# The GELU branch of a recurrent mixer, computed token-major and placed between convolution tiles

## The chip, the cores and the metric

The kernel runs on one core of one Trainium2 chip. The metric is the device time of one execution in microseconds (us). Five engines each run their own queue of instructions in order: TensorE (PE: matmuls; PEld are its weight loads), VectorE (DVE), ScalarE (ACT), GpSimd (POOL) and SyncE (SP, which issues the DMA transfers here).

## The reference

An encoder trunk of two residual layers on 256 tokens of width 2048, in float32. Layer 0 mixes tokens with grouped-query attention, layer 1 with the recurrent block that the change concerns; behind each stands a gated feed-forward of width 5632.

```python
def recurrent_mixer(h, w_in, conv_w, conv_b, w_a, b_a, w_i, b_i, lam, w_out):
    xy = h @ w_in
    xb, yb = jnp.split(xy, 2, axis=-1)
    yb = jax.nn.gelu(yb, approximate=True)
    xb = depthwise_conv_centred(xb, conv_w, conv_b)
    h_fwd = rg_lru(xb, w_a[0], b_a[0], w_i[0], b_i[0], lam[0], reverse=False)
    h_bwd = rg_lru(xb, w_a[1], b_a[1], w_i[1], b_i[1], lam[1], reverse=True)
    out = (h_fwd + h_bwd).astype(h.dtype) * yb
    return out @ w_out
```

`rg_lru` takes the convolved branch `x` through two block-diagonal products with biases (blocks of 256 channels) to the gates r and i, forms a = sigmoid(lam)^(8 r) and u = sqrt(1 - a^2) (i x), and runs h_t = a_t h_(t-1) + u_t over the tokens, forward and backward.

## The kernel before

Matmuls run on pairs of tiles: each float32 operand is split into a rounded part `hi` and the rest `lo`, and three products (hi hi, hi lo, lo hi) make one float32 product. Weights come in halves of a tile, 128 x 1024 elements: SP loads `raw`, ACT casts it to `hi` (L116), DVE subtracts to `lo` (L117). There are five buffers of each. The list `order` fixes the sequence of all halves, and each call of `half()` loads the next.

A product is made in one of two layouts. Feature-major (`project_sum`): the weights are the stationary operand, the 256 tokens move, so that a matmul has 256 columns; the result has one feature per partition, as convolution, gates and scans over the tokens need it (48 matmuls for a tile of 128 features). Token-major (`project_tokens`): the activations are stationary and 512 features move ("wide", 96 matmuls for the two accumulators of a group of 512 features); the feed-forward and the output projections use it. Its results are turned back by 32 x 32 transposes on DVE and moves between partitions (`turned`).

The PE program is written out in code order. Besides the main stream there is a list of things to be done later: each group of matmuls calls `step()`, which advances a count, and `later(n, fn)` runs `fn` when the count has advanced by n, one at each step. In the feature-major tiles a step is three matmuls; in the token-major ones three wide matmuls make two steps. The order on ACT, DVE, POOL and SP is not written out: a scheduler puts it together from the program with a timeline of its own, and it is fixed once the kernel is built.

The recurrence has eight blocks of 256 channels (two tiles). Loop b projects and convolves the two x tiles of block b+1 (`conv_branch`: `cb` is the projection times the norm's factor, then one activation on ACT (L671) and three taps and a split on DVE end in `xs`), then projects the two GELU tiles of block b (`gelu_branch`). Among these stand, by the table `WHEN`, the rest of block b: the gates (`gates`, 12 matmuls each that read `xs`, then sigmoids and tanh), `decay` (exponentials and squares), `scan` (square root and scan), the GELU's table function, and `finish` (product and split into the operand tile `g_t` of the output projection). `WHEN_LAST` does it for the last block, where nothing is convolved any more. The first convolution is done by `project_two`, whose last quarter comes after both tiles' first parts. The norm's factor per token is brought to all partitions by `spread` with a small matmul (L336), `NORM` steps after it is asked for. The output projection (`output`) takes four column groups of eight halves; in the first, the last half is run after the pending work is flushed.

In the attention the last three heads have delays of their own (`LATE`), and the last one uses DVE in place of POOL.

Of the kernel before, what the change touches and what calls it, by code (L numbers as in the profile page):

```python
# [12 lines left out]
F32 = mybir.dt.float32  # L13
F32R = mybir.dt.float32r
# [18 lines left out]
COMMON = {"sq", "nsq", "nr", "nrt", "rsq_s", "nj", "ndg", "nrb"}  # L33
# [6 lines left out]
NORM = 26  # L40
# [29 lines left out]
def trunk(ctx, tc, w, out):  # L70
# [56 lines left out]

    def ffn_order(l):
# [82 lines left out]
    def project_tokens(xs, ready=0, close=None):  # L211
        accs = [new_acc() for _ in range(2)]
        for k0 in range(0, len(xs), 2):
            if close is not None and k0 == ready:
                flush()
                close()
            half()
            hi, lo = (t.rearrange("p (k c) f -> p k (c f)", k=2) for t in newest["tiles"])
            end = k0 + 2 == len(xs)
            for k, a in ((0, 0), (1, 0), (0, 1), (1, 1)) if end else ((0, 0), (0, 1), (1, 0), (1, 1)):  # L220
                xh, xl = (xs[k0 + k][:, o + a * P : o + (a + 1) * P] for o in (0, S))
                for n, (x, wt) in enumerate(((xh, hi), (xh, lo), (xl, hi))):
                    pe.matmul(  # L223
                        accs[a], x, wt[:, k, :], start=(k0 + k == 0 and n == 0), stop=(end and k == 1 and n == 2)
                    )
                step()
                step()
        return accs
# [16 lines left out]


    def project_two(xs, late):
        banks = [new_acc() for _ in range(2)]
        for t in banks:
            sums(t[:, :S], half(), xs, 0)  # L250
        rest = [half() for _ in range(2)]
        n = len(xs) - HALF - late
        for t, wt in zip(banks, rest):
            sums(t[:, :S], wt[:n], xs, HALF)
        for t, wt in zip(banks, rest):
            sums(t[:, :S], wt[n:], xs, HALF + n)
            yield t[:, :S], t[:, S:]
# [37 lines left out]
    class Norm:  # L295
# [17 lines left out]
        def add(self, c):  # L313
            for a in range(2):
                act.activation(tmp("nj", (P, WIDE), bufs=1), x_tok[:, a, c, :], AF.Square, accum_out=self.sums[:, a, c : c + 1])
            for f in turned(x_tok[:, :, c, :]):
                self.operand(f, True)
# [25 lines left out]

    def turned(src):
        b = fp[0].tile([P, 2, FOUR, P], F32, tag="tb", name=nm("tb"))
        f = fp[0].tile([P, 8, FOUR, 32], F32, tag="tf", name=nm("tf"))
        for a in range(2):
            dve.transpose(b[:, a, :, :], src[:, a, :])  # L348
# [27 lines left out]
    def output(xs, norm=None, end=False, ready=0, close=None):  # L376
        for c in range(NCOL):
            accs = project_tokens(xs, ready, None if c else close)
            for a, acc in enumerate(accs):
                n = 2 if end and c == NCOL - 1 else 1  # L380
                for i in range(n):
                    sl = slice(i * WIDE // n, (i + 1) * WIDE // n)
                    y = x_tok[:, a, c, sl]
                    dve.tensor_tensor(y, y, acc[:, sl], ALU.add)
                    if end:
                        sync.dma_start(out=out[:, a, c, sl], in_=y)
            if norm is not None:
                norm.add(c)
        if norm is not None:
            norm.finish()  # L390
# [137 lines left out]
    def attend(h, acc, dst):  # L528
        late = h >= NQ - 1
        eng = dve if late else pool  # L530
        d_sum, d_sc, d_turn, d_val = LATE[h - NQ] if h >= NQ - 3 else USUAL if h else FIRST_HEAD
# [3 lines left out]
        rope_sum(y, rope[0], q, eng)  # L535
# [16 lines left out]
        def scores():  # L552
# [16 lines left out]
            for a in range(2):  # L569
                eng.tensor_scalar(pr[:, a, :], pr[:, a, :], rs[:, a : a + 1], 1.0, ALU.mult, ALU.mult)  # L570
# [25 lines left out]
    def act_tile():  # L596
        return xp.tile([P, 2 * S], F32R, tag="act", name=nm("act"), bufs=18)
# [34 lines left out]
    output(o_t, nf, ready=KT - 2, close=end_attention)  # L632
# [31 lines left out]
    def conv_branch(ct, accs):  # L664
        acc, run = accs
# [36 lines left out]
    class Block:  # L702
        def __init__(self, b):
            self.b = b
            self.eng = pool if b < NBLK - 1 else dve
            self.xcs, self.ys = [], []
            self.gate, self.th, self.hs = {}, {}, {}

        def gelu(self):
            for y in self.ys:  # L710
                table_act(y, y, AF.Gelu_apprx_tanh)
# [43 lines left out]
        def finish(self, j):  # L755
            y = self.ys[j]
            dve.tensor_tensor(y, self.hs[j], y, ALU.mult)
            split(g_t[2 * self.b + j], y)
# [3 lines left out]
    blk = nxt = None  # L762
    for b in range(-1, NBLK):
        blk, nxt = nxt, Block(b + 1) if b + 1 < NBLK else None
        if blk:
# [3 lines left out]
            work += [blk.gelu] + [partial(blk.finish, j) for j in range(2)]  # L769
# [9 lines left out]
        if blk:  # L779
            blk.ys = [gelu_branch(2 * b + i) for i in range(2)]  # L780
# [8 lines left out]
    output(g_t, nf, ready=KT - 2, close=end_recurrence)  # L789
# [86 lines left out]
```

## Time and profile before

| | |
|---|---|
| median of 3 runs | 2037.25 us (2036.8 to 2037.25) |
| profiled execution | 2036.59 us, span 2034.8 us |
| busy: PE, DVE, ACT, POOL | 2021.0, 1311.9, 1157.2, 168.6 us |
| mean granted clock of TensorE | 0.998 |
| DMA | 386.02 MB, mean 190 GB/s |
| the recurrent mixer, from its first convolution to the start of its output projection | about 985.8 to 1225.9 us |

Times on the timeline count from the span's start. A row of it gives the start, the length, the engine, the line and the tile written and those read. A stretch gives busy time and number of instructions of PE, PEld, DVE, ACT and POOL, the clock granted to TensorE as a share of full speed, the share of the DMA engines and GB/s. The program's names are those of the code: `acc` and `pm` are accumulators, `xg` normed inputs, `act` operand tiles of the output and down projections.

### The profile page before, as it was taken

Reading aid. Unit: us, or ns where it says so; the run is one execution under the profiler, and the core shown is the slowest. Engines: PE = TensorE matmul, PEld = TensorE weight load, DVE = VectorE, ACT = ScalarE, POOL = GpSimd, SP = SyncE. Lnnn points to the kernel's source line nnn. Section 1 sums busy time; section 2 is a strip of 40 time slices with the busy share of each in tenths; the row PEclk is TensorE's granted clock in tenths of the full one; section 3 lists DMA queues with packets and bytes.
Section 4 is the critical chain, followed back from the end, with each engine's and each line's share of the span. In section 5 each row is a group of like instructions: output and inputs, shape, how many; then the busy total and the mean of one; then the engine's idle time right before and its main releaser. Section 6 shows DMA issues by size and latency. Waiting matters only on the chain.

```text
span 2034.8 us, 27445 instructions
## 1 busy us (share of the span) xinstructions
PE 2021.0 (99%) x10124; PEld 1722.5 (85%) x10124; DVE 1311.9 (64%) x1899; ACT 1157.2 (57%) x1776; POOL 168.6 (8%) x213
## 2 busy tenths in 40 slices
PE   9999999999999999999899999999999999999999
PEld 8898888888888888888799998888888888888887
DVE  7998765654665445667778987765555556555553
ACT  7665755544555345556689987755435554355442
POOL 1563000000000000000134330000000000000000
PEclk9999999999999999999999999999999999999999
DMA  8444565665666656666556555566666666666664
GB/s 319 157 135 145 186 202 193 186 203 191 187 197 197 195 195 193 186 199 196 188 165 188 187 157 194 180 205 197 190 194 195 193 190 196 196 189 195 197 202 129
DMA packets 108998, 386.02 MB, mean 190 GB/s; under 512 B 12224, under 2 KB 12992, under 8 KB 108736
## 3 DMA queue, kind: packets, MB, share of 16 engines
q1 hardware_dynamic: 108720, 384.26, 59.7%
q8 instruction: 79, 1.29, 0.3%
q14 instruction: 55, 0.45, 0.1%
q10 hardware_dynamic: 144, 0.02, 0.0%
HBM read 382.13 MB, written 2.10 MB: 189 GB/s over the span
## 4 chain that ended last, share of the span: by engine, by line
PE 54%; issue 40%; DVE 2%; DMA 2%; ACT 1%; POOL 0%; SPq 0%; DVEq 0%; POOLq 0%
PE acc L223 40%; PE acc L201 3%; PE acc L231 3%; PE acc L232 3%; PE acc L233 3%; PE pm L232 1%; PE pm L233 1%; PE pm L231 1%; DVE lo L117 1%; DMA x_tok<-in_xt_dram 1%; DMA graw<-in_w_gates_dram 0%; DMA raw<-in_w_k_dram 0%; PE pm L576 0%; DMA raw<-in_w_qv_dram 0%; ACT hi L116 0%
## 5 line engine op out<-in xcount | busy, mean ns | idle before, releaser
L117 DVE TENSOR_TENSOR lo<-raw,hi 128x1024 fp32r<-128x1024 f32 (+1 forms) x708 | 868.7, 1230 | 665.5 <-ACT hi L116 657.1
L116 ACT CAST hi<-raw 128x1024 fp32r<-128x1024 f32 (+1 forms) x708 | 739.4, 1047 | 751.7 <-PE acc L223 744.0
L223 PE MATMUL acc<-hi,xg 128*128 128x512 f32 x2816 | 867.8, 389 | 0.0
L223 PEld LDWEIGHTS acc<-hi,xg 128*128 128x128 f32 x2816 | 528.6, 188 | 109.6
L223 PE MATMUL acc<-hi,act 128*128 128x512 f32 x1920 | 594.2, 389 | 0.0
L223 PE MATMUL acc<-lo,xg 128*128 128x512 f32 x1408 | 547.7, 389 | 0.0
L223 PEld LDWEIGHTS acc<-hi,act 128*128 128x128 f32 x1920 | 360.4, 188 | 74.4
L223 PE MATMUL acc<-lo,act 128*128 128x512 f32 x960 | 373.5, 389 | 0.0
L223 PEld LDWEIGHTS acc<-lo,xg 128*128 128x128 f32 x1408 | 264.3, 188 | 54.9
L223 PEld LDWEIGHTS acc<-lo,act 128*128 128x128 f32 x960 | 180.2, 188 | 37.1
L231 PE MATMUL acc<-xg,hi 128*128 128x256 f32 x512 | 145.0, 283 | 0.0
L232 PE MATMUL acc<-xg,hi 128*128 128x256 f32 x512 | 145.0, 283 | 0.0
L233 PE MATMUL acc<-xg,lo 128*128 128x256 f32 x512 | 144.7, 283 | 0.0
L201 PE MATMUL acc<-xg,hi 128*128 128x512 f32 x384 | 125.8, 396 | 0.2 <-ACT hi L116 0.2
L354 ACT COPY tf<-tb 32x256 f32<-32x256 f32 x272 | 109.8, 404 | 3.7 <-DVE tb L348 0.2
L231 PEld LDWEIGHTS acc<-xg,hi 128*128 128x128 f32 x512 | 98.3, 192 | 0.0
L232 PEld LDWEIGHTS acc<-xg,hi 128*128 128x128 f32 x512 | 98.2, 192 | 0.1
L233 PEld LDWEIGHTS acc<-xg,lo 128*128 128x128 f32 x512 | 98.2, 192 | 0.0
L201 PEld LDWEIGHTS acc<-xg,lo 128*128 128x128 f32 x384 | 71.8, 188 | 16.0 <-DVE lo L117 1.9
L201 PE MATMUL acc<-xg,lo 128*128 128x256 f32 x384 | 84.8, 288 | 0.5 <-DVE lo L117 0.4
L356 DVE COPY tf<-tb 32x256 f32<-32x256 f32 x272 | 77.2, 284 | 4.0
L667 POOL MEMSET cb<- 128x2 f32 x16 | 1.7, 108 | 823.1 <-PE acc L233 811.6
(172 smaller groups left out, 1324.5 us busy)
## 6 DMA issues: line engine op xcount, KB each, us to landing
raw<-in_w_gate_dram SPq DMA_DIRECT2D x176, 512.0 KB, 4.0
raw<-in_w_up_dram SPq DMA_DIRECT2D x176, 512.0 KB, 3.9
raw<-in_w_down_dram SPq DMA_DIRECT2D x176, 512.0 KB, 3.8
raw<-in_w_in_dram SPq DMA_DIRECT2D x64, 512.0 KB, 4.3
raw<-in_w_qv_dram SPq DMA_DIRECT2D x40, 512.0 KB, 4.2
raw<-in_w_o_dram SPq DMA_DIRECT2D x32, 512.0 KB, 3.6
raw<-in_w_out_dram SPq DMA_DIRECT2D x32, 512.0 KB, 4.0
graw<-in_w_gates_dram SPq DMA_DIRECT2D x32, 256.0 KB, 3.4
```

The costliest lines, as they stand in the source:

```text
L116: newest["cast"] = act.copy(hi[:, sl, :], raw[:, sl, :])
L117: dve.tensor_tensor(lo[:, sl, :], raw[:, sl, :], hi[:, sl, :].bitcast(F32), ALU.subtract)
L201: pe.matmul(o, w, x, start=(k == 0 and not part), stop=(k == total - 1 and not part))
L223: pe.matmul(accs[a], x, wt[:, k, :], start=(k0 + k == 0 and n == 0), stop=(end and k == 1 and n == 2))
L231: pe.matmul(o, hi, x[:, :S], start=start, stop=False)
L232: pe.matmul(o, hi, x[:, S:], start=False, stop=False)
L233: pe.matmul(o, lo, x[:, :S], start=False, stop=stop)
L354: act.copy(o, y)
L356: dve.tensor_copy(o, y)
L667: pool.memset(b[:, 0:2], 0.0)
```

## The change

1. The GELU branch becomes token-major: `w_y`, the second half of `w_in`, is laid out in groups of 512 features, projected by the new class `Columns` (`project_tokens` in resumable form), and given the norm's factor in the activation. Its result is turned by two DVE transposes and 16 small DMAs on SP for each group. The multiplication by `nr.r` on DVE goes.
2. The first group is projected ahead of everything, before the first convolution; the others in two halves, each at the start of a loop, ahead of the convolution tiles of the next block. `project_two` goes.
3. In the loop of the last block but one, the half column is the first of the output projection; both output projections begin two column groups (seven halves each) before the pending work is flushed.
4. `LATE` goes; `NORM`, the tables `WHEN` and `WHEN_LAST`, some buffers and the order of weights are adapted.

```diff
-COMMON = {"sq", "nsq", "nr", "nrt", "rsq_s", "nj", "ndg", "nrb"}
+COMMON = {"sq", "nsq", "nr", "nrt", "rsq_s", "ndg", "nrb"}
-NORM = 26
+NORM = 30
-LATE = ((17, 22, 15, 12), (10, 23, 15, 13), (7, 16, 16, 9))
+GELU = 9
-WHEN = (18, 25, 32, 39, 42, 46, 50, 54, 58, 60, 62, 64, 66, 70, 74)
-WHEN_LAST = (5, 9, 13, 17, 19, 20, 21, 24, 24, 25, 26, 27, 33, 39, 39)
+WHEN = (18, 25, 32, 39, 42, 46, 50, 54, 58, 60, 62, 64, 70, 74)
+WHEN_LAST = (18, 24, 30, 36, 38, 40, 42, 44, 48, 49, 50, 51, 62, 66)
...
-    order += wide("w_o") + ffn_order(0)
-    for b in range(-1, NBLK):
-        xin = range(2 * b + 2, 2 * b + 4) if b + 1 < NBLK else []
-        yin = range(KT + 2 * b, KT + 2 * b + 2) if b >= 0 else []
-        both = [halves(w["w_in"][c], KT) for c in (*xin, *yin)]
-        order += [t[i] for i in range(2) for t in both] if b < 0 else sum(both, [])
-    order += wide("w_out") + ffn_order(1)
+    order += out_order("w_o") + ffn_order(0)
+    columns, last = wide("w_y"), out_order("w_out")
+    order += columns[: KT // 2]
+    for b in range(NBLK):
+        order += sum((halves(w["w_in"][2 * b + i], KT) for i in range(2)), [])
+        order += columns[KT // 2 + 4 * b :][:4] if b < NBLK - 2 else last[:4] if b == NBLK - 2 else []
+    order += last[4:] + ffn_order(1)
...
+    class Columns:
+        def __init__(self, xs):
+            self.xs, self.k = xs, 0
+            self.accs = [new_acc() for _ in range(2)]
+
+        def run(self, n=None):
+            xs = self.xs
+            for k0 in range(self.k, self.k + 2 * n if n else len(xs), 2):
+                half()
...
+                    for i, (x, wt) in enumerate(((xh, hi), (xh, lo), (xl, hi))):
+                        pe.matmul(
+                            self.accs[a], x, wt[:, k, :],
+                            start=(k0 + k == 0 and i == 0), stop=(end and k == 1 and i == 2),
+                        )
+                    step()
+                    step()
+                self.k += 2
+            return self.accs
...
-    def output(xs, norm=None, end=False, ready=0, close=None):
+    def output(xs, norm=None, end=False, begun=(), close=None):
+        if close:
+            n = KT // 2 - 1
+            begun = [t.run(n - t.k // 2) and t for t in begun or [Columns(xs)]]
+            begun.append(Columns(xs))
+            begun[1].run(n)
+            flush()
+            close()
         for c in range(NCOL):
-            accs = project_tokens(xs, ready, None if c else close)
+            accs = (begun[c] if c < len(begun) else Columns(xs)).run()
...
-        late = h >= NQ - 1
-        eng = dve if late else pool
-        d_sum, d_sc, d_turn, d_val = LATE[h - NQ] if h >= NQ - 3 else USUAL if h else FIRST_HEAD
+        d_sum, d_sc, d_turn, d_val = USUAL if h else FIRST_HEAD
...
-    def gelu_branch(ct):
-        acc, y = project_sum(nr.xs)
-        if ct >= KT - 2:
-            y = tmp("gl")
-        dve.tensor_tensor(y, acc, nr.r, ALU.mult)
-        return y
+    def gelu_branch(accs):
+        y = tmp("gl", (P, 2, WIDE))
+        for a, acc in enumerate(accs):
+            table_act(y[:, a, :], acc, AF.Gelu_apprx_tanh, scale=nr.rt[:, a : a + 1])
+        b = tmp("tb", (P, 2, FOUR, P), bufs=1)
+        turn(b, y)
+        f = y.rearrange("p a (q k t) -> p (a q) k t", q=4, k=FOUR)
+        for q in range(4):
+            for i in range(4):
+                sync.dma_start(
+                    out=f[32 * i : 32 * i + 32, q::4, :, :].rearrange("f a k t -> f a (k t)"),
+                    in_=b[32 * q : 32 * q + 32, :, i, :],
+                )
+        gelu_t.extend(f[:, :, k, :] for k in range(FOUR))
...
-            y = self.ys[j]
-            dve.tensor_tensor(y, self.hs[j], y, ALU.mult)
-            split(g_t[2 * self.b + j], y)
+            h, n = self.hs[j], 2 * self.b + j
+            y = h.rearrange("p (q t) -> p q t", t=32)
+            dve.tensor_tensor(y, y, gelu_t[n], ALU.mult)
+            split(g_t[n], h)
...
+    gelu_branch(project_tokens(nr.xs))
+    blk = nxt = cols = first = None
...
+            if b == NBLK - 2:
+                first = Columns(g_t)
+                first.run(4)
+            elif b < NBLK - 2:
+                cols = Columns(nr.xs) if b % 2 == 0 else cols
+                cols.run(4)
+                if b % 2:
+                    later(GELU, partial(gelu_branch, cols.accs))
         if nxt:
-            accs = (project_sum(nr.xs) for _ in range(2)) if blk else project_two(nr.xs, FOUR)
-            nxt.xcs = [conv_branch(2 * b + 2 + i, t) for i, t in enumerate(accs)]
+            nxt.xcs = [conv_branch(2 * b + 2 + i) for i in range(2)]
...
-        if blk:
-            blk.ys = [gelu_branch(2 * b + i) for i in range(2)]
...
-    output(g_t, nf, ready=KT - 2, close=end_recurrence)
+    output(g_t, nf, begun=[first], close=end_recurrence)
```

What stands around the second block's gates on each engine follows, of before and of the change.

On PE, at gate 0 of the second block (`pm` is the gate's accumulator, `xs` the two convolved tiles). Before, ahead of it stands the convolution of the third block (`acc_1789` is its second tile):

```order
L233 MATMUL acc_1789_9359<-xg_1553_8102,lo_1792_9362 128x256
L231 MATMUL acc_1789_9359<-xg_1554_8105,hi_1791_9361 128x256
L232 MATMUL acc_1789_9359<-xg_1554_8105,hi_1791_9361 128x256
L233 MATMUL acc_1789_9359<-xg_1554_8105,lo_1792_9362 128x256
L231 MATMUL pm_1793_9372<-xs_1722_8944,ghi_1729_8974 128x256
L232 MATMUL pm_1793_9372<-xs_1722_8944,ghi_1729_8974 128x256
L233 MATMUL pm_1793_9372<-xs_1722_8944,glo_1728_8973 128x256
L231 MATMUL pm_1793_9372<-xs_1750_9092,ghi_1729_8974 128x256
```

In the change:

```order
L229 MATMUL acc_1742_9043<-hi_1811_9418,xg_1624_8479 128x512
L229 MATMUL acc_1741_9042<-hi_1814_9439,xg_1655_8654 128x512
L229 MATMUL acc_1741_9042<-lo_1815_9440,xg_1655_8654 128x512
L229 MATMUL acc_1741_9042<-hi_1814_9439,xg_1655_8654 128x512
L242 MATMUL pm_1816_9447<-xs_1790_9294,ghi_1754_9103 128x256
L243 MATMUL pm_1816_9447<-xs_1790_9294,ghi_1754_9103 128x256
L244 MATMUL pm_1816_9447<-xs_1790_9294,glo_1753_9102 128x256
L242 MATMUL pm_1816_9447<-xs_1806_9393,ghi_1754_9103 128x256
```

Between the convolution that made `xs_1806` and this gate there are now 27 wide matmuls of a GELU column; before there were two GELU tiles and 54 matmuls of the next convolution.

On ACT, at the activation of the second block's second convolution tile (L671, `acc_1723`), before; `sg` and `pm` are the gates of the first block:

```order
L401 ACTIVATE pm_1736_9012<-sg1_1740_9031,cs_2356 128x256
L401 ACTIVATE sg1_1741_9034<-pm_1736_9012,pk_77 128x256
L401 ACTIVATE pm_1736_9012<-sg1_1741_9034,cs_2356 128x256
L116 CAST hi_1781_9280<-raw_1780_9279 128x1024
L671 ACTIVATE acc_1723_8947<-cb_1748_9083,pk_77 128x256
L698 CAST ghi_1744_9072<-graw_1745_9073 128x512
L401 ACTIVATE sg2_1746_9077<-pm_1742_9058,pk_77 128x256
L401 ACTIVATE sg2_1747_9080<-pm_1742_9058,pk_77 128x256
L698 CAST ghi_1757_9137<-graw_1758_9138 128x512
L401 ACTIVATE sg3_1759_9142<-pm_1755_9123,pk_77 128x256
L401 ACTIVATE sg3_1760_9145<-pm_1755_9123,pk_77 128x256
L401 ACT_TABLE_LOAD
```

In the change it is L678, `acc_1791`; `sq` are squares of the first block's decays, and the activations of `pm_1752` and `pm_1761` its square roots:

```order
L678 ACTIVATE acc_1773_9191<-cb_1788_9285,pk_77 128x256
L116 CAST hi_1823_9482<-raw_1822_9481 128x1024
L410 ACT_TABLE_LOAD
L410 ACTIVATE pm_1752_9089<-pm_1752_9089 128x256
L410 ACTIVATE pm_1761_9132<-pm_1761_9132 128x256
L116 CAST hi_1839_9551<-raw_1838_9550 128x1024
L678 ACTIVATE acc_1791_9297<-cb_1804_9384,pk_77 128x256
L116 CAST hi_1848_9606<-raw_1847_9605 128x1024
L410 ACTIVATE pm_1752_9089<-pm_1752_9089 128x256
L410 ACTIVATE pm_1761_9132<-pm_1761_9132 128x256
```

The activation moved from between the sigmoids of the first block's gates 1 and 2 to behind its table load for square roots and the first two of these.

On DVE, from `cb` of the same tile, before (L674 are the taps, L268 and L269 write `xs`):

```order
L669 TENSOR_TENSOR cb_1748_9083<-acc_1723_8947,nrb_1694_8806 128x256
L117 TENSOR_TENSOR lo_1782_9281<-raw_1780_9279,hi_1781_9280 128x1024
L674 SCALAR_TENSOR_TENSOR acc_1723_8947<-cb_1748_9083,pk_77,acc_1723_8947 128x256 x2
L674 SCALAR_TENSOR_TENSOR xc_1749_9087<-cb_1748_9083,pk_77,acc_1723_8947 128x256
L268 CAST xs_1750_9092<-xc_1749_9087 128x256
L269 TENSOR_TENSOR xs_1750_9092<-xc_1749_9087,xs_1750_9092 128x256
L684 TENSOR_TENSOR acc_1751_9095<-acc_1751_9095,nrb_1694_8806 128x256
L117 TENSOR_TENSOR lo_1785_9316<-raw_1783_9314,hi_1784_9315 128x1024
```

In the change, the end of the same way; eight rows (two `lo`, two scans, two taps and two others) stand between `cb` and the first row here. L759 is the product behind a square root, L762 and L764 are scans, L771, L266 and L267 with `act` the first block's finish:

```order
L681 SCALAR_TENSOR_TENSOR acc_1791_9297<-cb_1804_9384,pk_77,acc_1791_9297 128x256
L759 TENSOR_TENSOR pm_1761_9132<-pm_1761_9132,sg3_1782_9241 128x256
L771 TENSOR_TENSOR h_1800_9350<-h_1800_9350,gl_1707_8850 128x256
L117 TENSOR_TENSOR lo_1860_9680<-raw_1858_9678,hi_1859_9679 128x1024
L267 TENSOR_TENSOR xs_1790_9294<-xc_1789_9289,xs_1790_9294 128x256
L762 SCALAR_TENSOR_TENSOR h_1802_9371<-sg0_1757_9111,pm_1752_9089 128x256
L681 SCALAR_TENSOR_TENSOR xc_1805_9388<-cb_1804_9384,pk_77,acc_1791_9297 128x256
L764 SCALAR_TENSOR_TENSOR h_1803_9381<-sg1_1766_9154,pm_1761_9132 128x256
L266 CAST act_1663_8683<-h_1800_9350 128x256
L266 CAST xs_1806_9393<-xc_1805_9388 128x256
L267 TENSOR_TENSOR act_1663_8683<-h_1800_9350,act_1663_8683 128x256
L267 TENSOR_TENSOR xs_1806_9393<-xc_1805_9388,xs_1806_9393 128x256
```

Where the tile's steps stood together, scans and the finish of the block ahead now stand among them, up to the last row, which writes the second half of `xs_1806`.

More of the change, by code (lines that the diff above doesn't have):

```diff
@@ L126, in wide, with out_order @@
         return [(src[c, i], HALF) for c in range(src.shape[0]) for i in range(src.shape[1])]
+    def out_order(name):
+        t, n = wide(name), KT // 2
+        return t[: n - 1] + t[n : 2 * n - 1] + [t[n - 1], t[2 * n - 1]] + t[2 * n :]
     def ffn_order(l):
@@ L208, in project, with project_tokens @@
         return acc
[L211 to L228, printed above, removed]
+    class Columns:
[6 more added lines that the diff above has]
+                half()
+                hi, lo = (t.rearrange("p (k c) f -> p k (c f)", k=2) for t in newest["tiles"])
+                end = k0 + 2 == len(xs)
+                for k, a in ((0, 0), (1, 0), (0, 1), (1, 1)) if end else ((0, 0), (0, 1), (1, 0), (1, 1)):
+                    xh, xl = (xs[k0 + k][:, o + a * P : o + (a + 1) * P] for o in (0, S))
+                    for i, (x, wt) in enumerate(((xh, hi), (xh, lo), (xl, hi))):
[7 more added lines that the diff above has]
+            return self.accs
+    def project_tokens(xs):
+        return Columns(xs).run()
     def three(o, hi, lo, x, start, stop):
@@ L244, in project_sum @@
         return bank[:, :S], bank[:, S:]
[L247 to L257, printed above, removed]
     def evac(acc, tag, after=None):
@@ L314, in add @@
             for a in range(2):
-                act.activation(tmp("nj", (P, WIDE), bufs=1), x_tok[:, a, c, :], AF.Square, accum_out=self.sums[:, a, c : c + 1])
+                junk = fp[0].tile([P, WIDE], F32, tag="nj", name=nm("nj"), bufs=1)
+                act.activation(junk, x_tok[:, a, c, :], AF.Square, accum_out=self.sums[:, a, c : c + 1])
             for f in turned(x_tok[:, :, c, :]):
@@ L340, in spread, with turn @@
             later(NORM, stage)
+    def turn(b, src):
+        for a in range(2):
+            dve.transpose(b[:, a, :, :], src[:, a, :])
     def turned(src):
@@ L346, in turned @@
         f = fp[0].tile([P, 8, FOUR, 32], F32, tag="tf", name=nm("tf"))
-        for a in range(2):
-            dve.transpose(b[:, a, :, :], src[:, a, :])
+        turn(b, src)
         for q in range(4):
@@ L596, in act_tile @@
     def act_tile():
-        return xp.tile([P, 2 * S], F32R, tag="act", name=nm("act"), bufs=18)
+        return xp.tile([P, 2 * S], F32R, tag="act", name=nm("act"), bufs=16)
     o_t = [act_tile() for _ in range(NQ)]
@@ L631, in trunk @@
     nf = Norm("norm_ffn", 0)
-    output(o_t, nf, ready=KT - 2, close=end_attention)
+    output(o_t, nf, close=end_attention)
     def ffn(norm, nxt):
@@ L663, in trunk, with conv_branch @@
     scope.append(rt.enter_context(tc.tile_pool(name="rp", bufs=2)))
-    def conv_branch(ct, accs):
-        acc, run = accs
+    def conv_branch(ct):
+        acc, run = project_sum(nr.xs)
         b = tmp("cb", (P, S + 4))
@@ L705, in __init__ @@
             self.eng = pool if b < NBLK - 1 else dve
-            self.xcs, self.ys = [], []
+            self.xcs = []
             self.gate, self.th, self.hs = {}, {}, {}
-        def gelu(self):
-            for y in self.ys:
-                table_act(y, y, AF.Gelu_apprx_tanh)
         def gates(self, g):
@@ L768, in trunk @@
             work += [partial(blk.scan, *u) for u in units]
-            work += [blk.gelu] + [partial(blk.finish, j) for j in range(2)]
+            work += [partial(blk.finish, j) for j in range(2)]
             when = WHEN if nxt else WHEN_LAST
@@ L852 @@
         "w_o": _wide(inp["attn_w_o"][0]),
-        "w_in": _tiles(inp["rnn_w_in"][0]),
+        "w_in": _tiles(inp["rnn_w_in"][0][:, :D]),
+        "w_y": _wide(inp["rnn_w_in"][0][:, D:]),
         "w_out": _wide(inp["rnn_w_out"][0]),
```

6 lines of the change are left out of this document (3 added, 3 removed).

## The prediction

> **What bounds the kernel now.** I read the page's share of busy time first, then single matmuls on the timeline, then the waits of TensorE (PE).
>
> ```profile
> PE 2021.0 (99%) x10124; PEld 1722.5 (85%) x10124; DVE 1311.9 (64%) x1899; ACT 1157.2 (57%) x1776; POOL 168.6 (8%) x213
> ```
>
> PE is the bound, with room on the others. Since the lengths of matmuls overlap, their price is the spacing of their starts (columns: start, length, engine, line):
>
> ```profile
> 979.91 0.39 PE L223 MATMUL acc<-lo,act 128*128 128x512 f32 x1
> ...
> 980.59 0.39 PE L223 MATMUL acc<-lo,act 128*128 128x512 f32 x1
> ...
> 1129.02 0.28 PE L231 MATMUL pm<-xs,ghi 128*128 128x256 f32 x1
> ...
> 1157.69 0.28 PE L231 MATMUL pm<-xs,ghi 128*128 128x256 f32 x1
> ```
>
> Three 512-wide ("wide") matmuls take 0.68 us, 0.227 each. The last two rows are the first gate matmul of a block and that of the next. Between them lie two convolution tiles, two GELU tiles (48 each) and four gates (12 each), 240 matmuls of 256 columns in 28.67 us: 0.1195 each, without a wait. The waits (total, times, longest) are few:
>
> ```profile
> PE pm L336 <- DVE ndg L330: 2.3, 1, 2.3
> PE pm L232 <- DVE xs L269: 2.2, 2, 1.3
> PE pm L231 <- ACT hi L116: 2.2, 1, 2.2
> PE pm L232 <- DVE pT L580: 0.7, 1, 0.7
> PE pm L231 <- DVE qs L268: 0.3, 1, 0.3
> ```
>
> The first is the norm's spread ahead of the mixer, the next two are the first block's gates, the last two the attention's tail. Stretches around the first gates (busy time and count of PE, PEld, DVE, ACT, POOL; then the granted clock):
>
> ```profile
> 1007.00:1010.50 3.50, 0.41 (x2) 0.19 (x1) 3.50 (x7) 2.08 (x3) 1.88 (x3) 0.88 0.60 200
> 1010.50:1014.00 3.50, 2.04 (x6) 1.46 (x7) 3.46 (x9) 0.57 (x1) 0.14 (x2) 0.50 0.79 266
> 1014.00:1017.00 3.00, 3.00 (x18) 3.00 (x18) 1.41 (x4) 1.70 (x2) 1.28 (x3) 0.59 0.59 182
> 1017.00:1020.00 3.00, 3.00 (x28) 3.00 (x27) 0.33 (x1) 2.92 (x7) 0.26 (x1) 1.00 0.31 89
> ```
>
> Ten microseconds hold 26 matmuls where 84 fit: 6.9 us lost, and the clock at half for a while after.
>
> **Part by part.** *Count.* 768 matmuls of 256 columns become 384 wide ones: 768 x 0.1195 = 91.8 less 384 x 0.227 = 87.1, a gain of 4.7 us. The Trainium skill, "TensorE: Matmul & The Clock Gate", section "Back-to-back issue gap", gives an isolated gap of N/2.4 + 2.5 ns, 216 and 109 ns; by it the gain would be 0.8 us and the sum 3.9 higher. The rows above (227 and 119.5) decide.
>
> *First gates.* With the whole first GELU column and, behind the first convolution, half a column ahead of them, the 6.9 us goes. Late next is the first convolution's result itself, by the 5.0 us from `cb` to `xs` shown under rival A against 6.1 us of cover: about a microsecond to spare, so 0 to 1 may come back.
>
> *Spread.* Its matmul comes after wide matmuls now, at nearly the same time, but one weight cast more stands in its chain on ScalarE (ACT): between 0 and +1.3 us, I take +0.4. *Attention's tail.* Fourteen wide halves instead of seven cover the last head, whose special delays and DVE work are dropped: between -1.0 (the two waits) and +1, I take -0.9, since cover doubles.
>
> *The loop.* Here I expect the loss. A loop now has half a GELU column (48 wide, 10.9 us), two convolution tiles of the next block (96 x 0.1195 = 11.5) and four gates (5.7): 28.1 us from gate 0 to gate 0, if nothing waits. But gate 0 comes 18 steps into the loop, 27 wide matmuls or 6.1 us behind the end of the convolution it reads; before, two GELU tiles and a third of the next convolution, about 18 us, lay between. So I follow the convolution's result. From gate 0 of a block, PE ends gate 3 at 21 wide (4.8) + 21 convolution (2.5) + 48 gate matmuls (5.7) = 13.0 us. What follows on ACT stands in before's trace, gate 3 ending at 1142.23:
>
> ```profile
> 1142.23 0.28 PE L231 MATMUL acc<-xg,hi 128*128 128x256 f32 x1
> ...
> 1142.88 0.84 ACT L401 ACTIVATE sg<-pm,pk 128x256 f32<-128x256 f32 x2
> 1143.73 1.28 ACT L401 ACT_TABLE_LOAD   x1
> ...
> 1152.11 0.65 ACT L401 ACTIVATE pm<-pm 128x256 f32<-128x256 f32 x2
> ```
>
> The first two square roots end 10.5 us after gate 3. In the new order of ACT the same work stands there plus the activation of the next block's first convolution tile (0.5): they end at 24.0 us after gate 0. Behind them stand a weight cast (0.95) and only then the activation of the second tile. VectorE (DVE) has 20 instructions from the second tile's `cb` (excluded) to the end of its `xs`: 3 `lo`, 4 scans, 4 taps, 2 xs casts, 2 xs subtractions, 5 of the kind of L746. Their rows in the recurrence:
>
> ```profile
> L117 DVE TENSOR_TENSOR lo<-raw,hi 128x1024 fp32r<-128x1024 f32 x69 | 90.7, 1319 | 25.4 <-ACT hi L116 18.9 <-DMA graw<-in_w_gates_dram 6.5
> L674 DVE SCALAR_TENSOR_TENSOR acc<-cb,pk,acc 128x256 f32<-128x256 f32 x32 | 15.4, 481 | 0.3
> L268 DVE CAST xs<-xc 128x256 fp32r<-128x256 f32 x16 | 13.3, 833 | 0.3
> L746 DVE TENSOR_TENSOR pm<-pm,sg 128x256 f32<-128x256 f32 x32 | 12.7, 418 | 0.6 <-ACT pm L401 0.2
> L749 DVE TENSOR_TENSOR_SCAN h<-sg,pm 128x256 f32<-128x256 f32 x16 | 10.8, 676 | 0.0
> L269 DVE TENSOR_TENSOR xs<-xc,xs 128x256 fp32r<-128x256 f32 x16 | 9.7, 608 | 0.5
> ```
>
> By these means they are 3.96 + 2.70 + 1.92 + 1.67 + 1.22 + 2.09 = 13.6 us. But a queue advances by starts, which lie closer:
>
> ```profile
> 1241.06 0.42 DVE L757 TENSOR_TENSOR gl<-h,gl 128x256 f32<-128x256 f32 x1
> 1241.39 1.22 DVE L117 TENSOR_TENSOR lo<-raw,hi 128x1024 fp32r<-128x1024 f32 x1
> 1242.53 0.28 DVE L268 CAST act<-gl 128x256 fp32r<-128x256 f32 x1
> 1242.85 0.42 DVE L269 TENSOR_TENSOR act<-gl,act 128x256 fp32r<-128x256 f32 x1
> 1243.19 1.22 DVE L117 TENSOR_TENSOR lo<-raw,hi 128x1024 fp32r<-128x1024 f32 x1
> ```
>
> That is 0.33, 1.14, 0.32, 0.34: 0.08 less each, and casts and subtractions faster than the mean of `xs`; so 10.7 at the least. I take 11.0. `xs` is then ready at 24.0 + 0.95 + 11.0 = 36.0 us, and PE's queue, which is in order, stands at gate 0 from 28.1: a wait of 7.9 us. After blocks 1, 3 and 5 a GELU stands between gate 3 and the exponentials:
>
> ```profile
> L401 ACT ACTIVATE fg<-acc,nr x44: 682/690/692, 289.3 to 1922.2; 128x512 f32<-128x512 f32 x44
> L401 ACT ACT_TABLE_LOAD x32 | 41.1, 1283 | 0.6
> ```
>
> The table load and two of these are +2.7, and no weight cast ahead of the activation there is -0.95: 9.6 us. With four and three such loops, 4 x 7.9 + 3 x 9.6 = 60.4 us. The wait repeats, since the next chain starts from the gate that was late. Two microseconds either way in each loop make 46 to 79.
>
> *The clock.* In the stretches above a wait of about that length left PE at half clock: 18 matmuls in 1014 to 1017 where 25 fit, 0.85 us lost, and if PE had work through the 6 us from 1010.5 on, 3 us. I take 2 for each of the seven waits, 14 (6 to 21), all of it on the chain. The Trainium skill, same page, Part 1, has the clock halve after an idle window of about 3.4 us and come back after a busy one of that length; it speaks against the change, the 0.50 of the second stretch agrees, and by it each wait would cost 1.7 to 3.4.
>
> *The end of the recurrence.* Gate 0 of the last block and the writes of its two outputs:
>
> ```profile
> 1210.34 0.28 PE L231 MATMUL pm<-xs,ghi 128*128 128x256 f32 x1
> ...
> 1240.72 0.42 DVE L269 TENSOR_TENSOR act<-gl,act 128x256 fp32r<-128x256 f32 x1
> ```
>
> With the 1242.85 row above they end 30.8 and 32.9 us after gate 0. Then PE needed them about 34.6 us after it; now 93 wide and 48 gate matmuls, 26.8 us. The gates are spread by 1.9 us more, the GELU's table load and two activations (2.1) are gone from the chain: a wait of 4 to 6, I take 5 and 2 for the clock; ends 0 and 10.
>
> *Hidden.* The 64 small DMAs that turn the GELU result stand in SP's queue ahead of weight loads, and wait for two transposes; the loads run far ahead:
>
> ```profile
> raw<-in_w_in_dram SPq DMA_DIRECT2D x64, 512.0 KB, 4.3
> ```
>
> With five raw and five split buffers (ten halves, some 27 us) ahead of PE, 4.3 us to land is covered; where the cover fails, each of four columns adds up to 10 us. The 16 multiplies by `nr.r` that go (0.42 each) and the 8 transposes that come leave DVE about as before.
>
> **Sum.** The profiled execution took 2036.6 us (span 2034.8), 0.7 below the median of the runs. -4.7 - 6.9 + 0.4 - 0.9 + 60.4 + 14 + 7 = +69.3: 2106 us. With the terms' ends: 2078 to 2134.
>
> **Rivals.** *A, the convolution keeps pace (faster).* In before the second tile's `cb` to `xs` takes 5.0 us:
>
> ```profile
> 1138.75 0.42 DVE L669 TENSOR_TENSOR cb<-acc,nrb 128x256 f32<-128x256 f32 x1
> ...
> 1142.93 0.84 DVE L269 TENSOR_TENSOR xs<-xc,xs 128x256 fp32r<-128x256 f32 x1
> ```
>
> Were it so after the change, 6.1 us of wide matmuls would cover it and only gains remain: 2036.6 - 12.1 = 2025, or 2032 with the wait at the end. Against it: there no square root or scan stood ahead of it in ACT's and DVE's queues. 0.11. *B, part of a wait.* If ACT and DVE go through the block's work 4 us a loop faster than my sum, the waits are 33 us, mostly too short to halve the clock: about 2062, 2040 to 2078. From the same rows, but beyond their ends. 0.14. *C, weights starve as well.* SP's queue held by GELU's DMAs: up to +40, 2146. 0.03. *D, the change leaves the matmul time as it is* (wide ones no cheaper for their work): 4.7 us higher, inside the forecast. My forecast has 0.70, no measurable change 0.02.
>
> A measurement of this kernel tells about 0.2% (4 us) from no change. Faster takes A, 0.11; same 0.02; slower the rest, 0.87. To leave out no more than 2 in 10, the range takes in the upper part of B: 2056 to 2132.
>
> **What would show it.** PE's waits should list gate matmuls waiting for `xs` at L266/L267, seven times at 8 to 10 us, starts of gate 0 some 38 to 40 us apart, granted clock 0.5 behind each, and one wait of the first output column for `act`; the wait at the first block's gates should be gone. I am wrong if gate 0 follows gate 0 in 28 us, or if the second tile's activation runs ahead of the square roots.

## The result and the profile after

The changed kernel takes 2105.39 us (median of 4 runs, 2103.74 to 2106.39) against 2037.25 (median of 4 runs, 2036.8 to 2037.61): 1.0334 times as long, 95% interval 1.0316 to 1.0352. The forecast was 2106. Its profiled execution took 2104.99 us, with a span of 2103.1. Of all executions reported here one stands outside the ratios, one of six of the last experiment, which took 7091.87 us at a granted clock of 0.275.

Its share of busy time, from the page, and PE's waits (total, times, longest):

```profile
PE 2041.9 (97%) x9740; PEld 1716.8 (82%) x9740; DVE 1293.8 (62%) x1885; ACT 1153.6 (55%) x1764; POOL 172.4 (8%) x219
```

```profile
PE pm L242 <- DVE xs L266: 23.2, 12, 3.3
PE pm L243 <- DVE xs L267: 16.1, 9, 2.5
PE acc L229 <- DVE act L266: 9.4, 3, 7.3
PE pm L335 <- DVE ndg L329: 2.6, 1, 2.6
PE pm L243 <- DVE pT L587: 1.7, 2, 1.0
```

384 matmuls fewer, and two new waits at the top: gates for the split of the convolution (`xs`), 39.3 us, and the output projection for its operand (`act`). The first gate of block 2, behind block 1, an odd one, on the timeline of PE:

```profile
1096.76 0.39 PE L229 MATMUL acc<-hi,xg 128*128 128x512 f32 x1
1100.41 0.58 PE L242 MATMUL pm<-xs,ghi 128*128 128x256 f32 x1 [3.26 <-DVE xs L266]
1102.15 0.58 PE L243 MATMUL pm<-xs,ghi 128*128 128x256 f32 x1 [1.16 <-DVE xs L267]
...
1104.32 0.58 PE L242 MATMUL pm<-xs,ghi 128*128 128x256 f32 x1 [1.38 <-DVE xs L266]
1106.57 0.58 PE L243 MATMUL pm<-xs,ghi 128*128 128x256 f32 x1 [1.67 <-DVE xs L267]
```

PE arrives at 1097.0 and does not run freely before 1106.6, 9.6 us later. It waits four times: for the cast and the subtraction of either tile. What ACT did meanwhile:

```profile
1082.51 0.83 ACT L410 ACTIVATE sg<-pm,pk 128x256 f32<-128x256 f32 x2
1083.36 1.28 ACT L410 ACT_TABLE_LOAD   x1
1084.66 1.27 ACT L410 ACTIVATE gl<-acc,nr 128x512 f32<-128x512 f32 x2
1085.94 1.28 ACT L410 ACT_TABLE_LOAD   x1
...
1095.77 0.65 ACT L410 ACTIVATE pm<-pm 128x256 f32<-128x256 f32 x2
1096.31 0.57 ACT L678 ACTIVATE acc<-cb,pk 128x256 f32<-128x256 f32 x1
```

The second tile's activation (last row) comes right behind the first two square roots of the previous block, 13.8 us after that block's last sigmoids began; the GELU and its table load lie in between. Then DVE, the first row behind this activation and the last one of the way to `xs`:

```profile
1096.90 0.43 DVE L759 TENSOR_TENSOR pm<-pm,sg 128x256 f32<-128x256 f32 x1
...
1106.10 0.42 DVE L267 TENSOR_TENSOR xs<-xc,xs 128x256 fp32r<-128x256 f32 x1
```

That is 9.6 us of one queue without a gap, 20 instructions. Behind an even block it is DVE that holds the way back first: the last matmul of block 1's convolution starts at 1052.77, `cb` follows on DVE at 1055.83, behind a `lo`, taps of the first tile and the products of the square roots, and ACT, free by then, waits 0.45 us for it before the activation. From `cb` to the end of `xs` (1066.50) DVE again has 20 instructions without a gap, in 10.3 us.

Stretches at the end of the gate shown above and behind it (columns as before):

```profile
1104.00:1108.00 4.00, 2.01 (x7) 1.72 (x8) 3.35 (x9) 0.00 (x0) 1.29 (x1) 0.50 0.76 269
1108.00:1112.00 4.00, 4.00 (x17) 3.32 (x16) 0.65 (x2) 3.35 (x6) 1.28 (x1) 0.76 0.12 46
```

PE is busy from 1108 on, at half clock for about half of that stretch.

An account can be made from the starts of all matmuls on the timeline, each against the usual distance of its kind (the median: 0.227 us behind a matmul of 512 columns, 0.120 at 256 and 0.108 at 128, the same before and after). PE lost 15.3 us in all before and 88.4 after, +73.1; fewer matmuls give -5.0; together 68.1 us, where the spans differ by 68.3. In the stretch from 1000 to 1340 gaps of 0.3 us and more are 58.2 us (before 5.7), smaller ones, mostly matmuls at half clock, 20.2 (before 0.6).

### The profile page after: what moved, and what is told of

Same layout as the page of the kernel before. It is cut to its first block, busy times and chain, and to the rows that moved or that the text cites. A ratio compares the mean times of both kernels' runs of the same rounds, so it can differ in the third digit from the quotient of the medians.

```text
span 2103.1 us, 26705 instructions
## 1 busy us (share of the span) xinstructions
PE 2041.9 (97%) x9740; PEld 1716.8 (82%) x9740; DVE 1293.8 (62%) x1885; ACT 1153.6 (55%) x1764; POOL 172.4 (8%) x219
## 4 chain that ended last, share of the span: by engine, by line
PE 86%; DVE 6%; ACT 4%; issue 2%; DMA 1%; POOL 0%; SPq 0%; DVEq 0%; ACTq 0%; POOLq 0%
PE acc L229 77%; PE acc L205 4%; DVE lo L117 2%; ACT hi L116 1%; PE pm L243 1%; PE pm L244 1%; PE pm L242 1%; ACT L410 1%; ACT sg L410 1%; ACT sq L753 0%; DVE h L762 0%; DVE h L764 0%; PE acc L242 0%; PE acc L243 0%; DVE pm L759 0%
## 5 line engine op out<-in xcount | busy, mean ns | idle before, releaser
L229 PE MATMUL acc<-hi,xg 128*128 128x512 f32 x3072 | 956.4, 391 | 0.0
L229 PEld LDWEIGHTS acc<-hi,xg 128*128 128x128 f32 x3072 | 581.2, 189 | 121.1
L229 PE MATMUL acc<-lo,xg 128*128 128x512 f32 x1536 | 601.2, 391 | 0.0
L229 PEld LDWEIGHTS acc<-lo,xg 128*128 128x128 f32 x1536 | 290.6, 189 | 60.0
L205 PE MATMUL acc<-xg,lo 128*128 128x256 f32 x384 | 84.7, 288 | 0.6 <-DVE lo L117 0.6
L205 PEld LDWEIGHTS acc<-xg,lo 128*128 128x128 f32 x384 | 71.9, 188 | 15.8 <-DVE lo L117 1.6
L674 POOL MEMSET cb<- 128x2 f32 x16 | 1.7, 108 | 914.7 <-issue 806.2
L242 PE MATMUL acc<-xg,hi 128*128 128x256 f32 x256 | 72.4, 283 | 0.0
L243 PE MATMUL acc<-xg,hi 128*128 128x256 f32 x256 | 72.3, 283 | 0.0
L244 PE MATMUL acc<-xg,lo 128*128 128x256 f32 x256 | 72.3, 282 | 0.0
L242 PE MATMUL pm<-xs,ghi 128*128 128x256 f32 x128 | 41.0, 320 | 23.2 <-DVE xs L266 23.2
L205 PEld LDWEIGHTS acc<-xg,hi 128*128 128x128 f32 x384 | 60.7, 189 | 1.1 <-ACT hi L116 1.0
L715 ACT CAST ghi<-graw 128x512 fp32r<-128x512 f32 x32 | 19.7, 617 | 71.0 <-PE pm L243 35.7
```

The source lines that it names most:

```text
L205: pe.matmul(o, w, x, start=(k == 0 and not part), stop=(k == total - 1 and not part))
L229: pe.matmul(self.accs[a], x, wt[:, k, :], start=(k0 + k == 0 and i == 0), stop=(end and k == 1 and i == 2),)
L242: pe.matmul(o, hi, x[:, :S], start=start, stop=False)
L243: pe.matmul(o, hi, x[:, S:], start=False, stop=False)
L244: pe.matmul(o, lo, x[:, :S], start=False, stop=stop)
L674: pool.memset(b[:, 0:2], 0.0)
```

## Experiments

My theory: PE's in-order queue meets gate 0 before `xs` is ready, since the steps of `xs` stand in ACT's and DVE's queues behind the block before, and the gate is only 6 us behind the convolution. Rivals: ACT or DVE have too much work for a loop of 28 us, or the GELU's DMAs make weights late, so that no order would help.

### The wait taken away: gates on older data

```diff
...
-                    x = self.xcs[k][1]
+                    x = (self.xcs if b == 0 else blocks_xs[b - 1])[k][1]
```

> The changed kernel, but the gates of each block from the second on read the convolved tiles of the block before (the computation is changed: wrong x in the gates), with all instructions, queues and DMAs kept. My theory (PE waits at each block's first gates for xs, whose steps stand behind the block before's square roots and scans): the seven waits at gate 0 and the half clock behind them go, about 54 and 15 us, so 2030 to 2040 us. Rival, ACT or DVE cannot do a loop's work in 28 us, or weights are late: the waits move elsewhere and it stays above 2080.

Measured: 2047.34 us, 1.0053 times the kernel before (1.0036 to 1.0069). 58 us of the 68 go with one dependence. All instructions are kept, and so is the order on PE and, but for some twenty or thirty rows each, on ACT and DVE (the activation still stands behind the square roots); on GpSimd more rows changed place. So a loop's work fits into its matmuls, against the first rival; and PE lists no wait for weights in the loops, against the second. PE's waits:

```profile
PE acc L229 <- DVE act L266: 11.1, 3, 9.0
PE pm L335 <- DVE ndg L329: 2.6, 1, 2.6
PE pm L242 <- DVE h L764: 2.1, 2, 1.2
```

It missed its range by 7 us: the wait for `act`, which I had counted among the seven at gate 0, remains, and is longer. New is the third row: gate 0 needs an accumulator that the block before frees with its last scan (the code keeps tanh, square root and the product behind it in the gates' accumulators until then).

### The place changed: columns behind the convolution

The loop's half column is put behind the two convolution tiles, and the order of weights with it.

```diff
...
+        if nxt:
+            nxt.xcs = [conv_branch(2 * b + 2 + i) for i in range(2)]
...
+        if blk:
             if b == NBLK - 2:
                 first = Columns(g_t)
                 first.run(4)
...
-        if nxt:
-            nxt.xcs = [conv_branch(2 * b + 2 + i) for i in range(2)]
...
```

> The changed kernel with one move: in each loop the convolution of the next block first, the half GELU column behind it, as the GELU tiles stood before the change. Gate 0 then comes 17 us behind its convolution instead of 6. My theory: no wait at the gates, 2028 to 2038 us, the wait at the end of the recurrence (some 6 us) kept. Rival, the token-major GELU itself (its DMAs on SP, its transposes, its place in ACT's queue) is what delays: above 2060.

Measured: 2051.35 us, 1.0072 (1.0057 to 1.0087): 54 us less than the changed kernel. No wait for `xs` is left. It is above its range, because the output's first column now waits longer for the sixth block's operand (of blocks counted from 0), which I had not put in, and for weights:

```profile
PE acc L231 <- DVE act L268: 13.2, 3, 11.1
PE acc L246 <- DVE lo L117: 1.7, 3, 0.8
PE acc L244 <- ACT hi L116: 1.2, 1, 1.2
```

### The order in the queues changed: scans forced behind

PE keeps its order; the square roots and the products behind them are held until the next block's convolution has been issued. For this the table puts the scans 5 to 8 steps later and `finish` 1 to 4.

```diff
-WHEN = (18, 25, 32, 39, 42, 46, 50, 54, 58, 60, 62, 64, 70, 74)
+WHEN = (18, 25, 32, 39, 42, 46, 50, 54, 66, 67, 68, 69, 74, 75)
...
+            root = act.activation(th, th, AF.Sqrt)
+            table_op(root)
+            drive = dve.tensor_tensor(th, th, self.gate[2 + d, j], ALU.mult)
+            if self.b < NBLK - 1:
+                follow(root, newest["conv"])
+                follow(drive, newest["xs"])
```

> The changed kernel, PE's order and all gates in place, but the square roots and the products behind them are held back in ACT's and DVE's queues until the next block's convolution has been issued there. My theory: xs is ready at about 29.4 us after gate 0 instead of 36 (9 DVE rows instead of 20 behind the activation), so waits of 1 to 2 us after even blocks and 3 to 4 after odd, too short for half clock: 2040 to 2060 us. Rival, the distance of 6 us behind the convolution is what counts and the order in the two queues does not: as the changed kernel, above 2095.

Measured: 2074.30 us, 1.0184 (1.0169 to 1.0199). It lies between: 31 us less than the changed kernel, 14 above my range. The waits for `xs` fell from 39.3 us to 15.9:

```profile
PE acc L229 <- DVE act L266: 10.8, 3, 8.8
PE pm L243 <- DVE xs L267: 8.0, 9, 1.2
PE pm L242 <- DVE xs L266: 7.9, 8, 2.3
```

So 23 of the 39 us of these waits go with the queue order alone, while all 39 go with the longer distance of the run before: the two do not add, since either shortens the same wait. What is left here is the time that the convolution's own steps need beyond the short distance. The shorter waits still brought half clock (14.7 us in gaps under 0.3 us), which I had left out, as I had the 8.8 us for `act`.

### The gates moved: 16 steps later

```diff
...
-            when = WHEN if nxt else WHEN_LAST
+            when = WHEN_LAST if not nxt else WHEN if b == NBLK - 2 else [t + 16 for t in WHEN]
```

> The changed kernel with the tables of all blocks but the last two moved 16 steps later: gate 0 stands behind the half column, 11.5 us behind its convolution, and the square roots come after the next block's convolution. My theory: the waits of blocks 1 to 5 go, one or two at blocks 6 and 7 (whose tables are kept) stay: 2036 to 2052 us. Rival, a loop-carried chain of ACT and DVE longer than 28 us wherever the gates stand: above 2080.

Measured: 2068.89 us, 1.0159 (1.0143 to 1.0174), 17 us above the range. Moving the gates moves the chain with them:

```profile
PE pm L242 <- DVE xs L266: 14.5, 6, 7.1
PE acc L229 <- DVE act L266: 9.4, 3, 7.3
PE pm L243 <- DVE xs L267: 4.4, 6, 0.9
```

The 7.1 us is the block whose table was kept. Before the other gates a wait of 2 to 3.5 us stays: the activation still stands behind the exponentials of the block before. The rival named there, a chain longer than a loop wherever the gates stand, is right in part; its price, above 2080, was not reached.

### The output projection's wait

Both begun columns run six halves, then the seventh of each.

```diff
...
-            n = KT // 2 - 1
+            n = KT // 2 - 2
...
+            for t in begun:
+                t.run(1)
```

> The changed kernel with one edit: the output projection's first column stops ahead of the sixth block's operand (six halves of both columns, then the seventh of each). Theory in the prediction, that this operand and gate 0 of the last block are late together: the 7.5 us wait moves to gate 0, 2102 to 2107 us. Rival, a wait of its own: it goes, with its half clock 2094 to 2098 us.

Measured: 2104.35 us, 1.0331 (1.0315 to 1.0346), no gain. The wait for `act` went from 9.4 to 2.1 us, and the gates' waits took it:

```profile
PE pm L242 <- DVE xs L266: 26.8, 14, 3.3
PE pm L243 <- DVE xs L267: 18.6, 10, 2.5
PE acc L229 <- DVE act L266: 2.1, 2, 1.8
```

The last block's gate 0 and the operand of the block before were late together, as expected.

### The clock: PE kept busy while it waits

```diff
...
+            if g == 0 and 0 < b < NBLK - 1:
+                for _ in range(WARMUP):
+                    pe.matmul(warm[0].accs[0], zeros, x_tok[:, 0, 0, :], start=False, stop=False)
```

> The changed kernel with 8 float32 matmuls of 512 columns by a zero operand added ahead of gate 0 of blocks 1 to 6, which add nothing to the result and keep PE busy during the wait. If the half clock behind the waits costs what the prediction says (2 us each and more), 2087 to 2096 us in spite of 48 matmuls more; if it costs nothing, 2103 to 2110.

Measured: 2097.44 us, 1.0295 (1.0281 to 1.0309), 8 us less than the changed kernel though 48 matmuls more are run, and 1 us above the range for a clock that costs. The mean granted clock is 0.993 instead of 0.983, and between 1000 and 1340 us of the timeline 0.96 instead of 0.89. The filler covers the wait behind even blocks almost wholly and leaves 1.9 us of it behind odd ones:

```profile
PE pm L244 <- DVE xs L268: 5.9, 4, 1.9
```

The filler gives ACT and DVE nothing that would make `xs` ready sooner (behind block 0 PE runs freely 8.3 us after it arrives at the filler, where it took 7.5 without), so that what was gained is the clock's.

### Mended versions

The first has the columns behind the convolution and, besides, the seventh halves late (as above), `NORM = 44`, the three heads' `LATE` as before the change, and the last block's gates as early as before:

```diff
-WHEN_LAST = (18, 24, 30, 36, 38, 40, 42, 44, 48, 49, 50, 51, 62, 66)
+WHEN_LAST = (5, 9, 13, 17, 19, 20, 21, 24, 24, 25, 26, 27, 39, 39)
```

> Columns behind the convolution, and four more edits: the output projections run six halves of each of the two begun columns, then the seventh of each; the last block's gates start 5 steps into its loop instead of 18; the norm's spread 44 steps later instead of 30; the last three heads have their own delays again. My theory: from the run with the columns behind (2051) go 11 to 13 us of the wait for the sixth block's output, 3 to 6 at the end of the recurrence, 2.8 at the spread, 1 to 2 in the attention: 2028 to 2034, below the kernel before. Rival, the waits only move: 2040 or more.

Measured: 2037.69 us, 1.0003 (0.9995 to 1.0012), no difference from the kernel before, and 4 us above its range. The 68 us are gone, but the time does not fall below that of the kernel before, as was expected. One long wait is left, for the accumulator seen above, and besides some for weights:

```profile
1237.51 0.58 PE L245 MATMUL pm<-xs,ghi 128*128 128x256 f32 x1 [8.25 <-DVE h L769]
```

```profile
PE acc L247 <- DVE lo L118: 2.8, 5, 0.8
```

The same with the GELU's small DMAs issued by GpSimd:

> As the run before it in this group, but the 64 small DMAs of the GELU result are issued by GpSimd instead of SP. Theory that SP's queue, held some 10 us by them, made gate weights late (2.8 us of waits in the run with the columns behind): 2 to 4 us less than its sibling. Rival, they cost as much in another queue, or GpSimd's own work (gate products, lo of gate weights) gets late: equal or 5 us more.

Measured: 2037.25 us, 1.0000 (0.9991 to 1.0009): no difference, and 0.4 us less than its sibling where 2 to 4 were expected. The accumulator's wait is 4.7 us here, and a wait of 2.9 us for a `lo` has come ahead of it.

The second version has only half a GELU column ahead of the first convolution and every further half a loop later, so that the whole output projection is left to cover the end; the tables follow it:

```diff
-GELU = 9
+GELU = 1
...
-WHEN = (18, 25, 32, 39, 42, 46, 50, 54, 58, 60, 62, 64, 70, 74)
-WHEN_LAST = (18, 24, 30, 36, 38, 40, 42, 44, 48, 49, 50, 51, 62, 66)
+WHEN = (18, 25, 32, 39, 42, 46, 50, 54, 58, 60, 62, 64, 92, 96)
+WHEN_LAST = (30, 34, 38, 42, 44, 45, 46, 49, 49, 50, 51, 52, 64, 64)
...
-    gelu_branch(project_tokens(nr.xs))
-    blk = nxt = cols = first = None
+    cols = Columns(nr.xs)
+    cols.run(4)
+    blk = nxt = None
...
+            if nxt:
+                cols = Columns(nr.xs) if b % 2 else cols
+                cols.run(4)
+                if b % 2 == 0:
+                    later(GELU, partial(gelu_branch, cols.accs))
```

> As the fifth run (columns behind the convolution, end parts mended), but only half a GELU column ahead of the first convolution, each further half a loop later, so that the last half column stands in the loop of the last block but one and the whole output projection behind it; the last block's gates start at step 30, two operands are finished later. Theory that the 8.4 us wait left at the last block's gates is the chain of the two last blocks (about 62 us from gate 0 of the sixth block to the last operand against 55 us of matmuls in the fifth run, 65 here): 2026 to 2031 us, faster than the kernel before by 0.3 to 0.5%. Rival, the matmul time saved is always paid back by a wait elsewhere (first gates, accumulators, weights): 2036 or more.

Measured: 2030.46 us, 0.9968 (0.9956 to 0.9980), inside its range: 0.3% less than the kernel before, and the accumulator's wait is gone. PE's longest waits are weights:

```profile
PE acc L247 <- DVE lo L118: 3.4, 4, 1.3
PE acc L245 <- ACT hi L117: 1.1, 1, 1.1
```

And with the small DMAs on GpSimd:

> As its sibling, the GELU result's small DMAs issued by GpSimd. If SP's queue, held by them, makes weights late inside the loops: 2 to 4 us less than its sibling; if not, within 1 us or slower.

Measured: 2027.51 us (the median of all six), 0.9952 (0.9940 to 0.9965). The intervals of the two ratios overlap, but both hold the spread of the same runs of the kernel before. Set side by side, all five executions of this version within the ratio (2026.61 to 2028.76) lie below all five of its sibling (2029.79 to 2031.08): some 3 us less, which is what was expected if SP's queue makes weights late. The traces bear that cause out in part at most. PE's waits for `lo` and `hi` of the loops' weights sum to 4.5 us in the sibling and 3.1 here, but ACT's wait for the gates' weights is the same in both, first with SP, then with GpSimd:

```profile
ACT ghi L722 <- DMA graw<-in_w_gates_dram: 10.8, 5, 2.9
```

```profile
ACT ghi L722 <- DMA graw<-in_w_gates_dram: 10.5, 6, 2.1
```

So the gain is measured; that SP's queue, held by these DMAs, is its cause is not shown, and why the gates' weights come late in both stays open.

## Why the prediction was right, step by step

The sum was +69.3 us, the difference of the spans is 68.3. The mechanism came out as forecast: gate 0 waits for `xs` in six loops and the output in the seventh for the operand behind it, the second tile's activation stands behind the square roots, and the first gates' old wait is gone. Gate 0 follows gate 0 in 37.6 to 39.3 us, close to the 38 to 40 foretold, but for the first pair (30.2) and the last (43.6, with the output's wait in it). The terms agree less well than their sum: the loop was taken 6.0 us too high and the wait at the end about 1, the clock 3.6 too low, and the attention's tail and the first gates together 2.8 too low. That these errors cancel to 1 us is luck.

- **Count**, -4.7: the usual distances are the same before and after the change, so each wide matmul kept its price, and rival D falls; by them the term is -5.0. The isolated gap of the Trainium skill ("TensorE: Matmul & The Clock Gate", section "Back-to-back issue gap"), which would have left 0.8, does not hold for these matmuls: the medians are 0.227 and 0.120 us against its 0.216 and 0.109.
- **First gates**, -6.9: their waits are gone; from 1000 to 1050 the starts lose 1.6 us (before 7.3). These 1.6 us are half clock behind the spread's wait, which neither term had; in the runs with gates on older data and with the seventh halves late it does not come behind the same wait.
- **Spread**, +0.4: the wait for `ndg` is 2.6 us instead of 2.3.
- **Attention's tail**, -0.9: wrong in sign. Up to 220 us PE lost 8.6 us before and 9.2 after, and the wait for `pT` is 1.7 instead of 0.7. The step that failed is "cover doubles": the waits lie inside a head, between its softmax and its values, where the wider cover at the end does not reach, and the heads' own delays that had shortened them were dropped (with them back, in the first mended version, it is 0.7 again).
- **The loop**, 60.4: the mechanism was right. From PE's arrival until it runs freely it is 7.5 us behind even blocks (7.9 in the sum) and 9.6 behind odd ones (9.6). The size came out 54.4 by starts: 6.8 and 8.85 us lost at the six gates, three each, and 7.5 at the output. Most of the 6.0 us between, some 4.4, is work that I took for waiting: the gate's first matmuls run as soon as the first tile is there. Most of the rest comes from the DVE list behind even blocks, counted as in the sum: 10.3 us measured where I took 11.0, below even my lower end of 10.7. Behind odd blocks two errors cancel: the list behind the activation has one `lo` fewer and takes 9.6 us, and it starts about as much later, since one more weight cast and the activation itself stand there on ACT. The upper end of 79 is a slip: 2 us in each of seven loops make 74, with which the terms' ends give 2076 to 2134. The seventh wait came at the output's first column; the run with the seventh halves late moves it to gate 0, where I had put it.
- **The clock**, 14, and 2 at the end: gaps under 0.3 us rose by 19.6 us in the recurrence, the end included, so about 2.4 for each of eight waits where I took 2. Filler matmuls bought back 8 us net of their own excess.
- **The end**, 5 and 2: the waits there sum to 2.8 us (0.30, 1.76, 0.74 in the three rows below), and the starts lose 6.1 us from 1300 on, clock included.

```profile
1326.67 0.47 PE L229 MATMUL acc<-hi,act 128*128 128x512 f32 x1 [0.30 <-DVE act L266]
...
1329.75 0.50 PE L229 MATMUL acc<-hi,act 128*128 128x512 f32 x1 [1.76 <-DVE act L266]
...
1331.22 0.79 PE L229 MATMUL acc<-hi,act 128*128 128x512 f32 x2 [0.74 <-DVE act L267]
```

- **Hidden**: no wait for weights in the loops of the changed kernel. With the waits gone, some appear (2.9 us in the run with the columns behind).

Rivals: A fell, since ACT's and DVE's queues did hold the convolution back. B fell, since the two go through a loop's work less than 1 us faster than in the sum, not 4. C fell: PE lists no wait for weights in the loops. That the same token-major GELU gives 2037.69 us once its pieces stand elsewhere and the ends are mended, and 2030.46 in the second version, shows that the loss lies in the order, and not in the layout.

## What to carry to other kernels

When a consumer is moved nearer to its producer in the queue of the bound engine, follow the producer's whole way through the other queues in their new order, and ask whether the next turn's way begins at this turn's end: then a wait repeats in every loop. Put independent matmuls between producer and consumer, and keep some for the end, where the last chain has no other cover. Taking one wait away often uncovers the next one at the same place, so test a cure with all its neighbours.

## What was not expected

Gate 0 also depends on the block before through the accumulators: with the `xs` wait gone it waited for the last scan to free one, 8.25 us in the first mended version. Instructions on DVE follow each other faster than their lengths say: the 20 behind an even block took 10.3 us, where their lengths in the same trace sum to 11.9, and the means that I used gave 13.6, since the casts and subtractions of `xs` were longer before the change (means of 833 and 608 ns, 279 and 492 after). Eight float32 matmuls by a zero operand, put into each of six waits, shortened the program by 8 us without making anything ready sooner.
